# Order on three queues written out from a project's last two tiles to the next swiglu's first pair, at two borders; modulation off late tiles

## The chip, the cores and the metric

The kernel runs on one core of a Trainium2 chip. A core has five engines that run their own queues of instructions and meet at semaphores: PE (TensorE, matrix products out of SBUF into PSUM), DVE (VectorE), ACT (ScalarE), POOL (GpSimd) and SP (SyncE, which here issues the DMAs that bring the weights). The metric is the device time of one execution in microseconds; lower is better. Every time below is in microseconds unless it is marked ns.

## What is computed

The reference is a two-layer transformer on 256 tokens with 256 context tokens beside them, model width 1024, everything in float32. Layer 0 is a half-weighted swiglu, a short convolution mixer and another half-weighted swiglu; layer 1 is the same with attention in the place of the convolution. Each of the six blocks is preceded by a normalisation with modulation and followed by a gated addition:

```python
mod = (jax.nn.silu(c) @ mod_w[i] + mod_b[i]).reshape(bsz, 3, 3, 1, D_MODEL)
h = _rms(t, g) * (1 + scale) + shift           # before each block
y = (jax.nn.silu(gte) * up) @ w2               # gte, up = split(h @ w13), 2816 wide each
lat = lat + 0.5 * mod[:, 0, 2] * y             # a swiglu; a mixer has no 0.5
```

The context tokens go through layer 0 and the first swiglu of layer 1 as well, so up to there every product has 512 columns: 256 tokens (half 0) and 256 context tokens (half 1).

## The kernel before, in words

**Number format.** Each float32 operand is split into a high part (rounded to the format PE multiplies in) and a low part (what is left). `split` (L107) makes both: ACT writes the high part (L108) and DVE subtracts it from the source for the low part (L109). A product is three matmuls (`mm3`, L127): high weight by high data, high weight by low data, low weight by high data (L131, L132, L133). Weights come in as raw float32 tiles `wr` of 128 x 1024, 512 KB each, from a ring of 8 buffers, and are split into `wh` and `wl`, rings of 4 (`half`, L111).

**Swiglu.** A swiglu has 22 hidden tiles of 128, in three thirds of 8, 7 and 7 (`ffn`, L754). In each third the hidden tiles are computed first and then `project` (L569) adds their share to the eight output tiles of x, one after the other. Most hidden tiles go by a scheme with seven block products in place of eight (`Pair`, L675): it needs sums of the data's blocks (T1 to T4, made by `Blocks.sums`, L399) and of the weights' blocks (S1 to S4, `Pair.sums`, L696). Per hidden tile that is `head` (A11 and A12 by the data's blocks), `five` (S1 by T1), `six` (S2 by T2, S4 by the block B11), `seven` (S3 by T3) and `four` (A22 by T4). The last two of a tile run among the products of the next tile.

**Normalisation.** x cannot be normalised before its last tile is added. `finish` (L547) adds a product to x (L553, DVE), `square_add` (L247) squares it on ACT and adds the squares up on DVE. For the last two output tiles, 6 and 7, `project` computes the 256 columns of half 0 first for both, and then half 1 (`late`), so that half 0 can be normalised while half 1 is multiplied. The sum over partitions, its root and the broadcast back are `rms_sum` (L268, L273, L277) and `rms_all` (L283). Then DVE scales a tile of x (L295), ACT adds the shift (L384 for the high part, L389 for a raw copy that the sums need) and DVE makes the low part (L385). `tail_norm` (L504) queues these steps in `pending`, which `flush` lets out between products.

**The borders.** Called border 1 below: from the convolution's output projection (`cw_out`) to layer 0's second swiglu. Border 2: from that swiglu to the first of layer 1. Border 3: from that one to attention. After borders 1 and 2 the first two hidden tiles are computed plainly (`w13_mm`, L634, half 0 of tile 0, half 0 of tile 1, then half 1 of both), because T1 to T4 are not there yet; the third is the first `Pair`.

**Modulation.** mod is computed on DVE out of weights that stream in: one unit (L173, `next_unit`, L200) multiplies a 128 x 1024 tile by silu(c) and sums it up, 224 units in all. `tick(n)` (L210) asks for n units after a tile: in `project` after each tile (1.5, 1.7 or 2), elsewhere by other numbers.

**What sets the order.** The kernel is traced into a tile framework, whose scheduler places the instructions on each engine's queue by its own estimate; it may move a unit of modulation to another place than its `tick`. Inside `tc.manual_schedule` the named engines take the instructions of the block in the order in which they are written; others may still be placed between them. `tc.issue_after(i)` keeps a block's instructions behind i on i's engine. Each engine works through its queue in order.

## Time and profile before

| | us |
|---|---|
| median of 3 runs | 1569.25 |
| the three runs | 1569.25, 1573.82, 1568.98 |
| the profiled execution, its time | 1571.47 |
| its span, first to last instruction | 1569.7 |
| PE busy | 1557.7 |
| DVE busy | 1333.4 |
| ACT busy | 733.8 |

The profile is one execution. A row of a timeline gives start, duration, engine, line, operation, output and inputs, shape, count, and in brackets the idle time ahead of it with what ended it. Instructions of an engine overlap: the next one starts before the last has ended, so the step from start to start is what an instruction costs its queue, and it is shorter than the duration. A matmul of 256 columns is such a case. PE's busy time is modelled from matmul ends. "PEclk" is the clock that was granted to PE as a share of full speed.

### The profile page before, as it was taken

The page shows a single profiled execution, that of the slowest core. Times are in us where ns is not written, and L with a number is a line of the kernel's source. Part 1 is how long each engine was busy: PE and PEld are TensorE (multiplying, and loading weights), DVE is VectorE, ACT ScalarE, POOL GpSimd, SP SyncE. Part 2 cuts the span into 40 slices and gives each one's busy share as a digit, 9 for nine tenths or more (in the row PEclk, how much of TensorE's full clock was granted, in tenths as well). Part 3 has the DMA queues.
Part 4 walks back from the last instruction along what each step waited for, and adds up shares of the span by engine and source line. Part 5 has one row for each costly group of instructions (what it writes and reads, how often), then busy time and mean ns, then how long its engine had stood idle before and what let it go on. Part 6 is the DMA issues. An engine that isn't in the chain of part 4 may idle for free.

```text
span 1569.7 us, 25671 instructions
## 1 busy us (share of the span) xinstructions
PE 1557.7 (99%) x10210; PEld 1422.0 (91%) x10210; DVE 1333.4 (85%) x2129; ACT 733.8 (47%) x1213; POOL 25.4 (2%) x20
## 2 busy tenths in 40 slices
PE   9999999999999999999999999999999999999999
PEld 7888998999888899989899899999899889898888
DVE  5998789899997698978989989969978887887676
ACT  5622452545322365435345465435345445674553
POOL 0000000000000000000000000000000002300000
PEclk9999999999999999999999999999999999999999
DMA  9675246355565323542533614533733853366562
GB/s 373 224 237 180 89 132 187 107 173 159 194 209 166 114 75 108 177 146 87 189 126 117 196 41 135 187 108 118 239 112 114 265 154 106 123 207 221 171 199 75
DMA packets 72120, 248.80 MB, mean 159 GB/s; under 512 B 9024, under 2 KB 10816, under 8 KB 72000
## 3 DMA queue, kind: packets, MB, share of 16 engines
q1 hardware_dynamic: 69408, 245.40, 48.0%
q10 hardware_dynamic: 2592, 1.76, 0.4%
q8 instruction: 80, 1.31, 0.3%
q14 instruction: 40, 0.33, 0.1%
HBM read 244.77 MB, written 1.05 MB: 157 GB/s over the span
## 4 chain that ended last, share of the span: by engine, by line
PE 88%; DVE 6%; DMA 2%; ACT 2%; issue 1%; POOL 0%; POOLq 0%; SPq 0%; ACTq 0%; DVEq 0%
PE py L131 8%; PE py L132 8%; PE py L133 8%; PE p L131 6%; PE p L133 6%; PE p L132 6%; PE q L133 5%; PE q L131 4%; PE q L132 4%; PE py L139 2%; PE pu L139 2%; PE pg L139 2%; PE pg L132 1%; PE pg L133 1%; DMA wr<-in_w 1%; PE pu L132 1%
## 5 line engine op out<-in xcount | busy, mean ns | idle before, releaser
L108 ACT ACTIVATE wh<-wr 128x1024 fp32r<-128x1024 f32 (+2 forms) x442 | 393.7, 916 | 361.9 <-PE py L132 119.6
L109 DVE TENSOR_TENSOR wl<-wr,wh 128x1024 fp32r<-128x1024 f32 (+2 forms) x442 | 454.5, 1048 | 95.1 <-ACT wh L108 76.2
L173 DVE CUSTOM_DVE_ANT_0 junk<-wr,scbc,modb 128x1024 bf16<-128x1024 f32 x218 | 279.4, 1282 | 15.2 <-DMA wr<-in_modT 13.1
L131 PE MATMUL py<-gh,wh 128*128 128x512 f32 (+1 forms) x570 | 214.7, 377 | 0.0
L132 PE MATMUL py<-gl,wh 128*128 128x512 f32 (+1 forms) x570 | 214.0, 375 | 0.0
L133 PE MATMUL py<-gh,wl 128*128 128x512 f32 (+1 forms) x570 | 213.9, 375 | 0.0
L133 PEld LDWEIGHTS py<-gh,wl 128*128 128x128 f32 x570 | 108.3, 190 | 19.0
L131 PEld LDWEIGHTS py<-gh,wh 128*128 128x128 f32 x570 | 108.5, 190 | 18.4
L132 PEld LDWEIGHTS py<-gl,wh 128*128 128x128 f32 x570 | 108.5, 190 | 18.2
L131 PE MATMUL p<-th,wh 128*128 128x256 f32 x432 | 122.3, 283 | 0.0
L132 PE MATMUL p<-tl,wh 128*128 128x256 f32 x432 | 122.3, 283 | 0.0
L133 PE MATMUL p<-th,wl 128*128 128x256 f32 x432 | 122.2, 283 | 0.0
L553 DVE SCALAR_TENSOR_TENSOR x<-py,G,x 128x256 f32<-128x256 f32 x189 | 83.5, 479 | 36.3 <-PE py L133 25.1
L133 PE MATMUL q<-bh,wl 128*128 128x256 f32 x320 | 91.5, 286 | 0.1
L131 PE MATMUL q<-bh,wh 128*128 128x256 f32 x320 | 90.9, 284 | 0.4 <-ACT wh L108 0.4
L132 PE MATMUL q<-bl,wh 128*128 128x256 f32 x320 | 90.5, 283 | 0.0
L132 PEld LDWEIGHTS p<-tl,wh 128*128 128x128 f32 x432 | 82.8, 192 | 0.3
L131 PEld LDWEIGHTS p<-th,wh 128*128 128x128 f32 x432 | 82.8, 192 | 0.3
L133 PEld LDWEIGHTS p<-th,wl 128*128 128x128 f32 x432 | 82.8, 192 | 0.0
L108 ACT ACTIVATE w4h<-wr 128x512 fp32r<-128x512 f32 x54 | 33.8, 625 | 75.1 <-DMA wr<-in_w 56.9
L108 ACT ACTIVATE gh<-gm 128x512 fp32r<-128x512 f32 x66 | 41.6, 630 | 56.0 <-DVE gm L751 53.8
L711 DVE TENSOR_TENSOR wr<-wr,wr 128x1024 f32<-128x1024 f32 x54 | 66.0, 1222 | 0.7
(303 smaller groups left out, 3946.3 us busy)
## 6 DMA issues: line engine op xcount, KB each, us to landing
wr<-in_w SPq DMA_DIRECT2D x176, 512.0 KB, 4.5
wr<-in_modT SPq DMA_DIRECT2D x122, 512.0 KB, 4.5
wr<-in_w2b SPq DMA_DIRECT2D x64, 448.0 KB, 3.9
wr<-in_w2a SPq DMA_DIRECT2D x32, 512.0 KB, 4.7
pm<-in_mod SPq DMA_DIRECT2D x16, 512.0 KB, 10.2
wr<-in_cw_cx SPq DMA_DIRECT2D x16, 512.0 KB, 4.7
wr<-in_cw_b SPq DMA_DIRECT2D x8, 512.0 KB, 4.4
wr<-in_cw_out SPq DMA_DIRECT2D x8, 512.0 KB, 3.9
```

Of the source, the lines that this page charges most:

```text
L108: nc.scalar.activation(out=hi, in_=src, func=AF.Copy)
L109: return nc.vector.tensor_tensor(out=lo, in0=src, in1=hi.bitcast(F32), op=ALU.subtract)
L131: nc.tensor.matmul(ps, wh, mh, start=first, stop=False, **kw)
L132: nc.tensor.matmul(ps, wh, ml, start=False, stop=False, **kw)
L133: nc.tensor.matmul(ps, wl, mh, start=False, stop=last, **kw)
L139: nc.tensor.matmul(ps, w[0], m[2], start=first and n == 0, stop=False)
L173: nc.vector.tensor_tensor_reduce(out=junk, in0=raw[j], in1=scbc[:, v, :], scale=1.0, scalar=modb[:, l, col : col + 1], op0=ALU.mult, op1=A ...
L553: nc.vector.scalar_tensor_tensor(out=x[:, m, s * S : s * S + S], in0=ps[:, o : o + S], scalar=g[:, m, s : s + 1], in1=x[:, m, s * S : s * ...
L711: tt(out=v(r2), in0=v(r2), in1=s2.unsqueeze(1).to_broadcast([P, 2, T2]), op=ALU.subtract,)
```

## The change

At borders 1 and 2 the order on PE, DVE and ACT is written out, from the product of output tile 6 up to the head of the first `Pair` (`enter`). `project` with `hold` returns a `Late` in place of its last two tiles; `enter` takes their steps one by one: `mm` a product, `x` the addition to x, `sq` and `acc` the square and its addition, `rms` the sum and root. `sc` scales a tile (DVE), `hr` and `hi` write its raw copy and its high part (ACT), `lo` its low part (DVE); `two` splits two tiles at once from the raw copy; `hi_of` and `lo_of` are the two halves of `split`. The first two hidden tiles of a swiglu run in pieces of some of their eight k. A later `Pair` makes its weights (`weights`) behind the block's last DVE instruction, `edge`. T3 and T4, made before ahead of the second `Pair`, are now made inside its `weights`, after its S1 and S2.

Besides: `project` calls `tick` for output tiles 0 to 5 alone (0 to 4 where the last two are late), with larger numbers (1.6 to 2.4). The 0.5 of a swiglu's gate moves into the modulation's units (`scale`, and `modb` halved once), which takes away four small multiplications, and a gate is asked for by output tile, so that only the units of the tiles so far have to be done. The table of silu is loaded by a small activation written into the order.

```diff
+    def hi_of(hi, lo, src):
+        nc.scalar.activation(out=hi, in_=src, func=AF.Copy)
+    def lo_of(hi, lo, src):
+        return nc.vector.tensor_tensor(out=lo, in0=src, in1=hi.bitcast(F32), op=ALU.subtract)
...
-            scale=1.0,
+            scale=0.5 if ch in (2, 8) else 1.0,
...
     def gate_of(l, j):
-        m = mod_ready(l, 3 * j + 2)
-        if j == 1:
-            return m
-        t = const.tile([P, KT, 2], F32, name=f"G{l}{j}", tag=f"G{l}{j}")
-        nv = 1 if (l, j) == (1, 2) else 2
-        nc.vector.tensor_scalar(
-            out=t[:, :, :nv], in0=m[:, :, :nv], scalar1=0.5, scalar2=None, op0=ALU.mult
-        )
-        return t
+        ch = 3 * j + 2
+        def get(m):
+            while done.get((l, ch), 0) < (m // 2 + 1) * 2 * streams(l, ch):
+                next_unit()
+            return modv[l, ch]
+        return get
...
             if n == 0:
                 tt(out=b11, in0=b12, in1=b11, op=ALU.subtract)
-                keep("T1", b11)
-            elif n == 1:
+                self.t["T1"] = hot("th"), hot("tl")
+                return *self.t["T1"], b11
+            if n == 1:
                 tt(out=b12, in0=b22, in1=b12, op=ALU.add)
+                return
+            if n == 2:
                 tt(out=b22, in0=b22, in1=b11, op=ALU.add)
-                keep("T2", b22)
-            else:
-                tt(out=b21, in0=b21, in1=b22, op=ALU.subtract)
-                keep("T3", b12)
-                keep("T4", b21)
+                self.t["T2"] = hot("th"), hot("tl")
+                return *self.t["T2"], b22
+            tt(out=b21, in0=b21, in1=b22, op=ALU.subtract)
+            keep("T3", b12)
+            keep("T4", b21)
...
+        def begin(self, s, A, B, ri):
+            self.par, self.ts = (A, B, ri), {}
+            for hf in range(2):
+                self.raw[hf, s] = hot("hr", F32)
+                self.t["B", hf, s] = hot("bh"), hot("bl")
...
+        def sc(self, s, *ks):
+            for k in ks:
+                self.ts[k] = scaled(s, k, self.par[0], self.par[2])
...
+        def hr(self, s, *ks):
+            for k in ks:
+                hf, c = self.cols(k)
+                self.put(s, k, self.raw[hf, s][:, c])
+        def hi(self, s, k):
+            hf, c = self.cols(k)
+            self.put(s, k, self.t["B", hf, s][0][:, c])
+        def lo(self, s, k):
+            hf, c = self.cols(k)
+            hi, lo = (t[:, c] for t in self.t["B", hf, s])
+            nc.vector.scalar_tensor_tensor(
+                out=lo, in0=self.ts[k], scalar=self.par[1][:, k, s : s + 1],
+                in1=hi.bitcast(F32), op0=ALU.add, op1=ALU.subtract,
+            )
+        def two(self, s, k, part):
+            hf, c = self.cols(k, 2)
+            t = self.t["B", hf, s]
+            (lo_of if part else hi_of)(*(u[:, c] for u in (*t, self.raw[hf, s])))
...
+    class Late:
+        def __init__(self, products, ws, nk, gate):
+            self.products, self.ws, self.nk, self.gate = products, ws, nk, gate
+            self.ps, self.parts = {}, {}
+        def mm(self, i, s, k0=0, k1=None):
+            if k0 == 0:
+                self.ps[i, s] = psum("py")
+            self.products(
+                self.ps[i, s], self.ws[i], range(k0, k1 or self.nk), s * S, s * S + S
+            )
+        def x(self, i, s):
+            finish(6 + i, self.ps[i, s], s * S, s * S + S, self.gate, None)
...
+        def rms(self, s):
+            return rms_sum(s, (accs[s], self.parts[1, s]))
...
-            tick(ev)
+            if m < (5 if late else 6):
+                tick(ev)
         if late:
             wl = [get(m) for m in (6, 7)]
             if tail:
                 ready()
+            if hold:
+                return Late(products, wl, nk, gate)
...
+        def own(self):
             ts = half()
             for i, key in enumerate(("A11", "A12")):
                 self.w[key] = [t[:, i * T2 : i * T2 + T2] for t in ts]
-                split(*self.w[key], self.raw[i][:, T2:])
+                yield *self.w[key], self.raw[i][:, T2:]
         def keep(self, keys, part):
-            hi, lo = half()
-            split(hi, lo, part)
+            ts = half()
             for i, key in enumerate(keys):
-                self.w[key] = [t[:, i * T2 : i * T2 + T2] for t in (hi, lo)]
+                self.w[key] = [t[:, i * T2 : i * T2 + T2] for t in ts]
+            return *ts, part
...
+        def sum1(self):
+            r1, r2 = self.raw
+            nc.vector.tensor_tensor(
+                out=r1[:, :T2], in0=r1[:, :T2], in1=r2[:, :T2], op=ALU.subtract
+            )
+        def sum2(self):
+            r1 = self.raw[0]
+            nc.vector.tensor_tensor(
+                out=r1[:, T2:], in0=r1[:, T2:], in1=r1[:, :T2], op=ALU.subtract
+            )
+            return self.keep(("S1", "S2"), r1)
...
+        def weights(self):
+            for t in self.own():
+                split(*t)
+            split(*self.sums(0))
+            if "T3" not in self.h.t and not isinstance(self.h, FirstBlocks):
+                self.h.sums(3)
+            split(*self.a22())
+            split(*self.sums(1))
...
+    def enter(late, l, b, h, gs):
+        A, B = scale_of(l, 2 * b), mod_ready(l, 6 * b)
+        src = a["w13"][l, b]
+        w = [load_w(src[0])]
+        raw = [load_raw(src[1, :, c : c + 1024]) for c in (0, 1024)]
+        pr = Pair(src[2], h)
+        gs.extend(new_pair("g") for _ in range(2))
+        pp = []
+        def g(i, s, k0, k1):
+            if (s, k0) == (0, 0):
+                pp.append((psum("pg"), psum("pu")))
+            w13_mm(pp[i], w[i], h, range(k0, k1), s * S, s * S + S)
...
+        queues = (nc.tensor, nc.vector, nc.scalar)
+        with tc.manual_schedule(engines={e.engine for e in queues}):
+            late.mm(0, 0)
+            late.x(0, 0)
+            late.sq(0, 0)
+            late.acc(0)
+            late.mm(1, 0)
+            late.x(1, 0)
+            late.sq(1, 0)
+            late.mm(0, 1, 0, 5)
+            ss = late.rms(0)
+            late.mm(0, 1, 5)
+            late.x(0, 1)
+            late.mm(1, 1, 0, 1)
+            ri = rms_all(*ss)
+            late.mm(1, 1, 1)
+            ts = [half() for _ in raw]
+            w.append(lambda o, wd=P: tuple(t[:, o % 1024 : o % 1024 + wd] for t in ts[o // 1024]))
+            w1 = [(*t, r) for t, r in zip(ts, raw)]
+            hi_of(*w1[0])
+            h.begin(0, A, B, ri)
+            h.sc(0, 0)
+            h.sc(0, 1)
+            h.hi(0, 0)
+            h.hr(0, 0)
+            h.lo(0, 0)
+            h.sc(0, 2)
+            h.hi(0, 1)
+            late.sq(0, 1)
+            h.hr(0, 1)
+            h.lo(0, 1)
+            late.acc(1)
+            late.x(1, 1)
+            h.sc(0, 3)
+            h.hi(0, 2)
+            late.sq(1, 1)
+            h.lo(0, 2)
+            h.hi(0, 3)
+            h.lo(0, 3)
+            h.hr(0, 2)
+            g(0, 0, 0, 3)
+            lo_of(*w1[0])
+            ss = late.rms(1)
+            g(0, 0, 3, 4)
+            h.hr(0, 3)
+            hi_of(*w1[1])
+            g(1, 0, 0, 1)
+            ri1 = rms_all(*ss)
+            g(1, 0, 1, 4)
+            h.sc(0, 4, 5)
+            h.hr(0, 4, 5)
+            h.two(0, 4, 0)
+            h.sc(0, 6, 7)
+            h.two(0, 4, 1)
+            h.hr(0, 6, 7)
+            h.two(0, 6, 0)
+            lo_of(*w1[1])
+            h.two(0, 6, 1)
+            g(0, 0, 4, 8)
+            silu()
+            g(1, 0, 4, 8)
+            h.begin(1, A, B, ri1)
+            h.sc(1, 0, 1)
+            h.hr(1, 0, 1)
+            h.two(1, 0, 0)
+            pr.sum1()
+            h.sc(1, 2, 3)
+            h.two(1, 0, 1)
+            h.hr(1, 2, 3)
+            h.two(1, 2, 0)
+            h.sc(1, 4, 5)
+            h.two(1, 2, 1)
+            g(0, 1, 0, 4)
+            h.hr(1, 4, 5)
+            h.two(1, 4, 0)
+            h.sc(1, 6, 7)
+            h.two(1, 4, 1)
+            h.hr(1, 6, 7)
+            h.two(1, 6, 0)
+            t1 = h.sums(0)
+            h.two(1, 6, 1)
+            g(0, 1, 4, 8)
+            hi_of(*t1)
+            a22 = pr.a22()
+            hi_of(*a22)
+            lo_of(*t1)
+            own = list(pr.own())
+            for o in own:
+                hi_of(*o)
+            h.sums(1)
+            t2 = h.sums(2)
+            for o in own:
+                lo_of(*o)
+            p0 = post(0)
+            hi_of(*t2)
+            s12 = pr.sum2()
+            hi_of(*s12)
+            g(1, 1, 0, 8)
+            p0 = mul(0, *p0)
+            lo_of(*t2)
+            lo_of(*s12)
+            lo_of(*a22)
+            hi_of(*p0)
+            s34 = pr.sums(1)
+            lo_of(*p0)
+            p1 = post(1)
+            hi_of(*s34)
+            lo_of(*s34)
+            p1 = mul(1, *p1)
+            pr.head()
+            hi_of(*p1)
+            pr.edge = lo_of(*p1).ins
+        return pr
...
                 if t == 0 and not gs:
-                    w = [load_w(a["w13"][l, b, 0])]
-                    gs = [new_pair("g") for _ in range(2)]
-                    pp = [(psum("pg"), psum("pu")) for _ in range(2)]
-                    w13_mm(pp[0], w[0], h, range(KT), 0, S)
-                    flush()
-                    w.append(load_w(a["w13"][l, b, 1]))
-                    w13_mm(pp[1], w[1], h, range(KT), 0, S)
-                    h.sums(0)
-                    w13_mm(pp[0], w[0], h, range(KT), S, T2)
-                    w13_post(pp[0], gs[0], 0, T2)
-                    heads.append(Pair(a["w13"][l, b, 2], h))
-                    h.sums(1)
-                    heads[0].sums(0)
-                    w13_mm(pp[1], w[1], h, range(KT), S, T2)
-                    w13_post(pp[1], gs[1], 0, T2)
-                    heads[0].head()
-                    h.sums(2)
-                    heads[0].sums(1)
+                    heads.append(enter(late, l, b, h, gs))
...
-                        pr.sums(0)
-                        pr.sums(1)
+                        with tc.issue_after(prev.edge) if prev and prev.edge else nullcontext():
+                            pr.weights()
...
+    for ch in (2, 8):
+        b = modb[:, :, ch * KT : ch * KT + KT]
+        nc.vector.tensor_scalar(out=b, in0=b, scalar1=0.5, scalar2=None, op0=ALU.mult)
...
-    ffn(0, 0, h, T2, lazy_gate(0, 0), tail_norm(0, 1, hn), gs0, 2)
+    ffn(0, 0, h, T2, gate_of(0, 0), tail_norm(0, 1, hn), gs0, (2.3, 2.1))
...
-    hn = Blocks()
-    project(
+    late = project(
         by_pairs("cw_out"), lambda k, c0, c1: (zs[k][0][:, c0:c1], zs[k][1][:, c0:c1]), KT,
-        lazy_gate(0, 1), tail_norm(0, 2, hn), T2, 2, 1.5,
+        gate_of(0, 1), tail_square, T2, 2, hold=True, ev=1.6,
     )
-    h = hn
-    hn = Blocks()
-    ffn(0, 1, h, T2, lazy_gate(0, 2), tail_norm(1, 0, hn), (), 1.7)
-    h = hn
+    late = ffn(0, 1, Blocks(), T2, gate_of(0, 2), tail_square, late=late, hold=True, ev=(2.3, 1.8))
     hn = Plain()
-    ffn(1, 0, h, T2, lazy_gate(1, 0), tail_norm(1, 1, hn), (), 1.5)
+    ffn(1, 0, Blocks(), T2, gate_of(1, 0), tail_norm(1, 1, hn), late=late, ev=(2.4, 1.9))
```

## The prediction, made before the changed kernel ran

> **What bounds the kernel now.** I read the page first, then the busy time of a few stretches, then the timelines of PE, DVE and ACT in them, and last the order in which the changed program stands on each queue.

> ```profile
> span 1569.7 us, 25671 instructions
> PE 1557.7 (99%) x10210; PEld 1422.0 (91%) x10210; DVE 1333.4 (85%) x2129; ACT 733.8 (47%) x1213; POOL 25.4 (2%) x20
> ...
> PE 88%; DVE 6%; DMA 2%; ACT 2%; issue 1%; POOL 0%; POOLq 0%; SPq 0%; ACTq 0%; DVEq 0%
> ...
> wr<-in_w SPq DMA_DIRECT2D x176, 512.0 KB, 4.5
> ```

> PE is busy all the time but 12.0 us, and the chain is PE's for 88%, with DVE next. So a change that leaves PE's matmuls alone can win only PE's waits. The next view has four stretches: border 1 from the first late product to the second pair, border 2 likewise, and border 3 in two parts. Columns: stretch, length, busy time (count) of each engine, clock, DMA.

> ```profile
> 547.50:600.00 52.50, 51.23 (x417) 50.09 (x416) 48.19 (x74) 33.53 (x58) 0.00 (x0) 1.00 0.26 82
> 900.60:950.00 49.40, 48.69 (x400) 47.85 (x399) 43.22 (x66) 34.58 (x59) 0.00 (x0) 1.00 0.18 59
> 1256.00:1260.00 4.00, 2.48 (x20) 2.27 (x19) 3.08 (x5) 0.42 (x1) 0.00 (x0) 0.96 0.39 124
> 1260.00:1267.00 7.00, 7.00 (x36) 7.00 (x36) 4.51 (x14) 2.93 (x6) 0.00 (x0) 0.54 0.43 128
> ```

> PE is idle for 1.27 at border 1 and 0.71 at border 2, while DVE is busy for 92% and 87%. DVE is the second bound there: whatever is put on it, or makes it wait, soon reaches PE. Border 3 costs more: 1.52 idle, and then 7.0 us at a clock of 0.54, which is 7.0 x 0.46 = 3.2 more.

> PE's timeline around three waits, with the steps that the sum needs:

> ```profile
> 573.62 0.28 PE L131 MATMUL pu<-bh,wh 128*128 128x256 f32 x1
> 573.74 0.28 PE L132 MATMUL pu<-bl,wh 128*128 128x256 f32 x1
> ...
> 574.34 0.28 PE L131 MATMUL pu<-bh,wh 128*128 128x256 f32 x1
> 575.63 0.39 PE L132 MATMUL pg<-bl,wh 128*128 128x256 f32 x1 [1.01 <-DVE bl L109]
> ...
> 943.29 0.39 PE L131 MATMUL q<-bh,wh 128*128 128x256 f32 x1 [0.39 <-ACT wh L108]
> ...
> 1258.60 0.38 PE L268 MATMUL ss<-ones,acc 128*128 128x1 f32 x2 [1.52 <-DVE acc L259]
> ```

> A matmul of 256 columns is a step of 0.12. The wait at 575.63 took 1.29 - 0.12 = 1.17 from PE, 0.16 more than its idle time; short waits show only in this way. With some eight waits at border 1 and six at border 2, I put what PE loses there now at 1.27 + 8 x 0.16 = 2.6 and 0.71 + 6 x 0.16 = 1.6 (estimates; the idle time alone is the low end). Together 4.2 is all that the written order can win.

> **The change part by part.** Steps from start to start, which the sums go by:

> ```profile
> 557.59 1.26 DVE L295 SCALAR_TENSOR_TENSOR t<-x,A,ss 128x256 f32<-128x256 f32 x3
> 558.76 0.87 DVE L385 SCALAR_TENSOR_TENSOR bl<-t,mod,bh 128x256 fp32r<-128x256 f32 x2
> ...
> 585.76 0.69 DVE L109 TENSOR_TENSOR gl<-gm,gh 128x512 fp32r<-128x512 f32 x1
> 586.37 1.22 DVE L109 TENSOR_TENSOR wl<-wr,wh 128x1024 fp32r<-128x1024 f32 x1
> 587.50 0.69 DVE L645 TENSOR_TENSOR gm<-sg,pu 128x512 f32<-128x512 f32 x1
> 588.10 1.22 DVE L109 TENSOR_TENSOR tl<-hr,th 128x1024 fp32r<-128x1024 f32 x1
> ...
> 1248.92 1.28 DVE L173 CUSTOM_DVE_ANT_0 junk<-wr,scbc,modb 128x1024 bf16<-128x1024 f32 x1
> 1250.13 0.08 DVE L173 DVE_READ_ACCUMULATOR2_ANT mod<- 128x1 f32 x1
> ...
> 562.02 1.05 ACT L108 ACTIVATE wh<-wr 128x1024 fp32r<-128x1024 f32 x1
> 562.97 1.29 ACT L389 ACTIVATE hr<-t,mod 128x256 f32<-128x256 f32 x3
> ...
> 556.53 0.71 PE L283 MATMUL ss<-ident,ri 128*128 128x128 f32 x4
> 557.00 0.36 PE L133 MATMUL py<-zh,wl 128*128 128x256 f32 x1
> ```

> DVE: 0.39 for 256 columns (1.17 for three), 0.61 for 512, 1.13 for 1024, 1.21 for a unit of modulation. ACT: 0.95 for a copy of 1024. The broadcast takes PE 0.47. Let B be the start of PE's product after the broadcast for half 0 (557.00 at border 1).

> *Same work.* PE has the same 9538 rows before and after, so its work costs 0. DVE has three splits of 1024 as six of 512, 6 x 0.61 - 3 x 1.13 = +0.3 per border, counted below. POOL is not touched.

> *Border 1, the head.* The written order puts the high copy of the second hidden tile's weights ahead of the first activation on ACT. Its buffer is that of the last projection weights, and in the built program it waits for the eighth product after B: B + 0.08 + 7 x 0.12 + 0.28 = B+1.2. The copy ends its step at B+2.2; the first high part then ends at B+2.7, and DVE's first low part at B+3.2. PE comes there at B + 0.08 + 21 x 0.12 = B+2.6. It waits for the high part and then for the low one, and for the third low part again, since DVE has by then to add x's last tile as well: 0.3 + 0.4 + 0.9, 1.7 with restarts. Bounds: 0 if the copy were early, 1.9 if it hides nothing. DVE stands still for 1.8 meanwhile. Before, ACT made the high parts first (next fence) and this copy at 562.02.

> ```profile
> 558.10 0.91 ACT L384 ACTIVATE bh<-t,mod 128x256 fp32r<-128x256 f32 x2 [1.82 <-DVE t L295]
> ...
> 570.47 2.83 DVE L295 SCALAR_TENSOR_TENSOR t<-x,A,ss 128x256 f32<-128x256 f32 x7 [2.50 <-PE ss L283]
> ...
> 591.09 1.22 DVE L109 TENSOR_TENSOR tl<-hr,th 128x1024 fp32r<-128x1024 f32 x1
> 592.65 2.43 DVE L109 TENSOR_TENSOR wl<-wr,wh 128x1024 fp32r<-128x1024 f32 x3 [0.35 <-ACT wh L108]
> ```

> *Border 1, the tail.* Before, DVE made T3 and T4 (588.10, 591.09) ahead of the second pair's weights (592.65). Now they stand behind them, behind `edge`, and behind a sum that waits for PE's S4 product. From B+0.3 to T3's low part DVE has 22 instructions of 256 columns, 21 of 512 and 12 of 1024: 8.6 + 12.8 + 13.6 = 35.0, so B+35.3 without a wait. PE comes to S3 by T3 after 192 products of the swiglu (23.0), twelve small matmuls of half 1 (estimate 1.4, at the broadcast's pace) and 84 products of the pairs (10.1): B+37.1. DVE may thus wait for 1.8 in all. I count 5.4: 1.8 at the head, 1.6 behind ACT's raw copies and high parts of half 0, 2.0 behind the high parts of S3/S4 and of the second hidden tile and behind S4. T3 is there at B+40.7; PE, already 1.7 late, wants it at B+38.8: 1.9. T4 and S1's low part follow, 2.27 against the 1.44 of twelve products: 0.8, of which the queue, with six to eight products of the next blocks put ahead, hides some 0.4. Sum 1.7 + 1.9 + 0.4 + 0.3 for restarts = 4.3, against 2.6 before: **+1.7** (from -2.6 if DVE waits for less than 1.8, to +3).

> *Border 2.* The copy waits for nothing here, since each projection weight has a buffer of its own and the one it takes is read for the last time before B. The head costs 0.5. But four units of modulation stand inside the block on DVE, two by T1 and T2 and two by S3/S4, moved there by the scheduler: 4 x 1.21 = 4.85. Their two loads stand in SP's queue ahead of the fifth tile's weights, so a sum of those, placed ahead of `edge`, waits for a load that starts when S3/S4 is made. It lands 4.5 later by the page's median, 3.56 of which DVE fills: up to 0.9, taken as 0.6. DVE to the second pair's first own weight: 8.6 + 18 x 0.61 + 10 x 1.13 + 4.85 + 0.3 = B+36.0, with waits of 1.9 behind ACT and this 0.6 B+38.5. PE comes at B + 0.08 + 18 x 0.12 + 23.0 + 1.4 + 60 x 0.12 + 0.5 = B+34.3: 4.2. To T3 there are 3 x 0.61 + 2 x 1.13 = 4.1 more against 2.9 of PE: 1.2; then 0.4 as above. Sum 0.5 + 4.2 + 1.2 + 0.4 + 0.2 = 6.5, against 1.6: **+4.9** (from -1.6 to +7).

> *Modulation.* All 224 units stay. At border 1 the four in the late tiles go; PE lost little by them, **-0.3**. At border 3 the order still shows four units at the same places, between the same loads: 0, though the change is described as taking them off. Elsewhere units move by a tile or two; PE's other waits are short, so 0, within 1 either way.

> *Gate and table.* Four small DVE multiplications less, two more; silu's table is loaded elsewhere on ACT. 0: ACT is 47% busy, and half 1's activations, next behind the load, are wanted some 4 us later.

> **Sum.** 1.7 + 4.9 - 0.3 = +6.3 on the profiled execution's 1571.47. That stands 2.2 above the median 1569.25; on the median the sum is **1575.6**.

> **The rivals.** *DVE keeps pace.* If its waits at the head are filled and the total stays below 1.8 at border 1 and its like at border 2, both borders' losses go: 1569.25 - 4.2 = 1565.1, faster. For it: DVE had 2.50 of idle time at 570.47 that the new order fills. Against it: the copy on ACT and the four units.

> *Border 3 clears.* If the modulation's loads land 1.5 earlier there, its 1.52 and 3.2 go: 1575.6 - 4.7 = 1570.9. Against it: the same places in both queues.

> *The clock halves at border 2.* Two waits of some 2 us lie 1.4 apart there, and border 3's row shows 0.54 after only 1.52 idle. That would cost up to 3.2: 1578.8. For it: that row. Against it: 1.01 idle at 575.63 left no mark, and DVE's lateness would cover part.

> [...]

> **How the numbers follow.** Forecast 0.50 (by itself 1572 to 1579), DVE keeps pace 0.20, border 3 clears 0.13, the clock 0.12, none of these 0.05. The range 1565 to 1580 takes in all four. This kernel's no change is within 0.3%, 1564.5 to 1574.0, about what a measurement can tell. Faster: half of the first rival and little else, 0.12. Same: its other half, border 3, and the forecast's low end, 0.28. Slower 0.60.

> **What would show it.** Right: at border 1 an ACT weight copy before the first high part, with DVE idle some 1.8; in both borders PE waits on `tl` (T3) and on the second pair's weights, about 2 at border 1 and 5 at border 2; four units between `hr` sums at border 2; the same stretch of low clock at border 3. Wrong: PE idle of less than 1 at either border, or DVE idle for long between T1 and T3.

## The result

The changed kernel takes 1582.01 us (median of 4 runs, 1580.04 to 1582.87), the kernel before 1569.55 beside it (4 runs, 1568.98 to 1573.82): ratio 1.0072, 95% interval 1.0052 to 1.0092. It is 12.5 slower, where 6.3 was forecast; 1582.01 lies above the range's 1580.

The page of the changed kernel, its profiled execution (1582.87):

```profile
span 1581.0 us, 25678 instructions
PE 1560.3 (99%) x10210; PEld 1421.9 (90%) x10210; DVE 1334.8 (84%) x2133; ACT 736.7 (47%) x1221; POOL 25.4 (2%) x20
...
PE 82%; DVE 11%; ACT 3%; DMA 3%; issue 1%; POOL 0%; POOLq 0%; ACTq 0%; DVEq 0%
```

The span is 11.3 longer, PE is busy for only 2.6 more, and DVE's share of the chain has gone from 6% to 11%: new waits of PE, mostly for DVE. The four stretches that answer to those of the prediction (stretch, length, busy time of PE, PEld, DVE, ACT, POOL with counts, clock, DMA share, GB/s):

```profile
549.80:604.90 55.10, 52.30 (x425) 51.06 (x424) 45.22 (x72) 33.75 (x61) 0.00 (x0) 1.00 0.17 58
906.20:961.00 54.80, 49.77 (x406) 48.62 (x405) 48.98 (x79) 35.09 (x62) 0.00 (x0) 1.00 0.22 72
1267.00:1271.50 4.50, 2.31 (x20) 2.11 (x18) 1.66 (x4) 0.27 (x1) 0.00 (x0) 1.00 0.49 187
1271.50:1278.00 6.50, 6.48 (x42) 6.48 (x43) 4.57 (x11) 3.35 (x7) 0.00 (x0) 0.74 0.46 164
```

PE is idle for 2.8 at border 1 and 5.0 at border 2; border 3 still has its wait (2.2) and a stretch of low clock behind it (0.74). PE's timeline at its longest waits:

```profile
565.76 0.39 PE L138 MATMUL pg<-bl,wh 128*128 128x256 f32 x1 [0.54 <-DVE bl L461]
...
601.14 0.39 PE L138 MATMUL p<-tl,wh 128*128 128x256 f32 x1 [1.90 <-DVE tl L109]
...
948.97 0.38 PE L137 MATMUL p<-th,wh 128*128 128x256 f32 x1 [1.88 <-ACT sg L841]
953.97 0.38 PE L139 MATMUL p<-bh,wl 128*128 128x256 f32 x1 [1.27 <-DVE wl L109]
958.04 0.39 PE L138 MATMUL p<-tl,wh 128*128 128x256 f32 x1 [1.43 <-DVE tl L109]
...
1271.52 0.38 PE L274 MATMUL ss<-ones,acc 128*128 128x1 f32 x2 [2.21 <-DVE acc L265]
```

Each takes 0.16 more from PE than its idle time, as in the prediction. To see where all of the 11.3 is, the trace's PE starts were added up by stage: the time from one start to the next, less the step of that form (0.120 for 256 columns, 0.227 for 512). What is left is PE's loss, in us. The same 560 matmuls stand for border 1 in every kernel, and so on; "half" is the part in which five or more matmuls in a row took about twice their step (0.21 where it is 0.120, as at 1273.70 in the changed kernel). Each row is one profiled execution; e1 to e12 are the runs below.

```
                 start  ffn00  conv  border 1    rest   border 2    rest  border 3    attn
                                     (half)     ffn01   (half)     ffn10  (half)
before           13.9   1.1    0.4   2.8         1.0    1.9         0.7   6.7 (2.7)   4.1
after            15.6   0.9    1.2   5.4         1.8    6.9         2.3   5.8 (1.2)   4.1
e1 order only    17.6   0.6    0.4   5.1         0.9    4.7         1.0   5.4 (0.9)   4.1
e2 modul. only   13.7   1.1    1.2   2.6         1.8    4.8         1.2   3.4         4.1
e3 bias late     13.7   1.0    1.2   7.6 (1.4)   2.4    7.4         1.5   5.4 (1.0)   4.1
e4 units out     14.2   0.6    1.2   5.7 (1.4)   2.0    4.5         2.0   7.0 (2.7)   4.1
e5 copy late     15.8   0.8    1.2   3.8         1.6    7.5         1.0   5.6 (1.2)   4.1
e6 T3 inside     15.7   1.1    1.2   5.4         2.7    9.7 (2.6)   2.5   3.2         4.1
e7 head first    13.8   1.4    1.2   5.8         1.7    7.2 (1.1)   1.1   3.4         4.1
e8 border 3      13.6   0.8    0.4   2.8         0.8    1.9         0.7   1.7         4.1
e9 T3 first      13.7   1.0    1.2   5.0         1.4    8.2 (1.5)   0.9   3.7         4.1
e10 border 0     15.8   1.1    0.1   6.3 (1.5)   1.8    8.8 (1.6)   0.9   5.4 (1.4)   4.1
e11 mended       15.7   0.6    0.4   4.1 (1.5)   2.9    4.6 (1.6)   1.0   1.7         5.4
e12 mended again 13.7   0.6    0.4   2.8         2.7    5.6 (1.6)   0.8   1.7         4.1
```

Before to after: border 1 +2.6, border 2 +5.0, and +3.2 in places that the forecast had at zero: the convolution +0.8, the rest of the two later swiglus +0.8 and +1.6. With the first swiglu's pairs (-0.2) that is 10.5 with the unrounded values. Start (+1.7) and border 3 (-0.9) vary between executions of one kind, as the runs show.

### The profile page after: what moved, and what is told of

It reads as the page before. It is cut to its first block, busy times and chain, and to the rows that moved or that the text cites. A ratio compares the mean times of both kernels' runs of the same rounds, so it can differ in the third digit from the quotient of the medians.

```text
span 1581.0 us, 25678 instructions
## 1 busy us (share of the span) xinstructions
PE 1560.3 (99%) x10210; PEld 1421.9 (90%) x10210; DVE 1334.8 (84%) x2133; ACT 736.7 (47%) x1221; POOL 25.4 (2%) x20
## 3 DMA queue, kind: packets, MB, share of 16 engines
HBM read 244.77 MB, written 1.05 MB: 155 GB/s over the span
## 4 chain that ended last, share of the span: by engine, by line
PE 82%; DVE 11%; ACT 3%; DMA 3%; issue 1%; POOL 0%; POOLq 0%; ACTq 0%; DVEq 0%
PE py L137 8%; PE py L138 8%; PE py L139 8%; PE p L137 5%; PE p L139 5%; PE p L138 5%; PE q L139 4%; PE q L137 3%; PE q L138 3%; DVE wl L109 3%; PE py L145 2%; PE pu L145 2%; PE pg L145 2%; ACT wh L108 1%; DMA wr<-in_w 1%
## 5 line engine op out<-in xcount | busy, mean ns | idle before, releaser
L108 ACT ACTIVATE wh<-wr 128x1024 fp32r<-128x1024 f32 (+2 forms) x430 | 383.4, 916 | 368.1 <-PE py L138 158.3
L109 DVE TENSOR_TENSOR wl<-wr,wh 128x1024 fp32r<-128x1024 f32 (+2 forms) x430 | 441.1, 1046 | 88.3 <-ACT wh L108 69.4
L607 DVE SCALAR_TENSOR_TENSOR x<-py,mod,x 128x256 f32<-128x256 f32 x213 | 94.2, 478 | 50.7 <-PE py L139 39.4
L795 DVE TENSOR_TENSOR wr<-wr,wr 128x1024 f32<-128x1024 f32 x54 | 65.9, 1221 | 0.9
L108 ACT ACTIVATE gh<-gm 128x512 fp32r<-128x512 f32 x62 | 39.0, 630 | 55.4 <-DVE gm L864 53.9
L139 PE MATMUL q<-th,wl 128*128 128x256 f32 x216 | 61.6, 285 | 1.2 <-DVE wl L109 1.1
## 6 DMA issues: line engine op xcount, KB each, us to landing
wr<-in_w SPq DMA_DIRECT2D x176, 512.0 KB, 4.3
wr<-in_modT SPq DMA_DIRECT2D x120, 512.0 KB, 4.6
wr<-in_w2a SPq DMA_DIRECT2D x32, 512.0 KB, 4.5
pm<-in_mod SPq DMA_DIRECT2D x16, 512.0 KB, 10.2
wr<-in_cw_cx SPq DMA_DIRECT2D x16, 512.0 KB, 4.6
wr<-in_cw_b SPq DMA_DIRECT2D x8, 512.0 KB, 4.4
wr<-in_cw_out SPq DMA_DIRECT2D x8, 512.0 KB, 3.8
```

Source lines behind the costliest of these rows:

```text
L108: nc.scalar.activation(out=hi, in_=src, func=AF.Copy)
L109: return nc.vector.tensor_tensor(out=lo, in0=src, in1=hi.bitcast(F32), op=ALU.subtract)
L139: nc.tensor.matmul(ps, wl, mh, start=False, stop=last, **kw)
L607: nc.vector.scalar_tensor_tensor(out=x[:, m, s * S : s * S + S], in0=ps[:, o : o + S], scalar=g[:, m, s : s + 1], in1=x[:, m, s * S : s * ...
L795: tt(out=v(r2), in0=v(r2), in1=s2.unsqueeze(1).to_broadcast([P, 2, T2]), op=ALU.subtract,)
```

## The experiments

### Which part of the change: e1, e2

e1 keeps the written order and takes the modulation's rates, rule, gates and halving back; e2 is the kernel before with that part of the change alone.

```diff
 e1, against the changed kernel
-            if m < (5 if late else 6):
-                tick(ev)
+            tick(ev)
...
-    late = ffn(0, 1, Blocks(), ..., late=late, hold=True, ev=(2.3, 1.8))
+    late = ffn(0, 1, Blocks(), ..., late=late, hold=True, ev=(1.7, 1.7))
 e2, against the kernel before
-            tick(ev)
+            if m < (5 if late else 6):
+                tick(ev)
```

> The written order alone, with the modulation's rates, gates and halving as they were before. The two theories share the table of what PE loses by stage (time from start to start beyond its own step): border 1 2.8 before and 5.4 after, border 2 1.9 and 6.9, start 13.9 and 15.6, the rest of the three swiglus and the convolution 3.3 and 6.2. Theory: the order by itself costs only DVE's lateness, and no unit of modulation stands in border 2's block here: border 1 5.4 to 5.9 (two units are back in its late tiles), border 2 2.0 to 2.6 (6.9 less the four units' 4.85), start 13.9, rest 3.3; about 1573, +3.3. Rival (the order itself is slow at border 2, and the units fill waits of DVE): border 2 5 to 7, about 1577.

> The modulation's part alone: rates, the rule that late tiles have no units, a gate made tile by tile, and the two halvings of the biases; the order at the borders is the scheduler's as before. Theory: the loss that the forecast had at zero comes from this part: start +1.7 (the halvings stand ahead of the first sum of squares on DVE), convolution and the rest of the two later swiglus +3.2, border 3 -0.9, border 1 -0.3; three units stand in border 2's block here too, +1.5 to +3.6. About 1574 to 1577. Rival (units cost nothing wherever DVE has spare time, and it is the written order that delays the tiles behind it): start +1.7 at most, elsewhere within 0.5, about 1570 to 1571.

e1: 1579.58 against 1569.71, ratio 1.0051 (1.0032 to 1.0070). e2: 1573.12, ratio 1.0019 (1.0006 to 1.0032). The stages of e1 are near the theory's for border 1 (5.1, where 5.4 to 5.9 was expected; four units are back there, not two) and right for the rest (as before), and wrong for border 2: 4.7, not 2.0 to 2.6. So the order alone costs 2.8 there, and two waits stay, on the second pair's weights and on T3. Its time is 6.6 above the theory's 1573: 2.1 to 2.7 of that is border 2, and its four executions had a mean clock of 0.9968 (the profiled one lost 17.6 at the start).

e2 is what the forecast missed: the modulation's part alone gives the convolution +0.8, the rest of the two swiglus +0.7 and +0.5, and +3.0 at border 2, where no order was written. Three units now stand among the steps of border 2 in the scheduler's order too (918.55, 926.51 and 944.03; before, none); what each costs there was not separated. The start did not lose the 1.7 that its theory said (13.7), border 3 fell further than its 0.9 (from 6.7 to 3.4, 2.7 of which is half clock), and the time, 1573.12, is below the theory's 1574 to 1577.

### The start: e3

```diff
         for step in FIRST_STEPS.split():
             steps[step[0]](*(int(c) for c in step[1:]))
+        for ch in (2, 8):
+            b = modb[:, :, ch * KT : ch * KT + KT]
+            nc.vector.tensor_scalar(out=b, in0=b, scalar1=0.5, scalar2=None, op0=ALU.mult)
...
-    for ch in (2, 8):
-        ...
```

> The changed kernel with the two halvings of the biases written behind the first block's steps. Theory: they delay the first sum of squares by 0.24, and the clock at the start falls for longer on that account (mean clock 0.79 to 0.87 from 10 to 20 us): start back to 13.9, 1.7 less, 1580.3. Rival (the clock at the start differs from run to run, whatever DVE does): start 15 to 16 again, 1582.

1583.66, ratio 1.0083 (1.0065 to 1.0101). The start came back to 13.7, as the theory has it, but e2 has 13.7 with the halvings in front, and e1 17.6 without any. So the rival holds: the start differs by execution. What differs is the clock: in the profiles with no half clock between 10 and 21 us the start loses 13.6 to 14.2, in those with 3.4 us of it 15.6 to 15.8, and in e1, with 6.8 us, 17.6. These are windows at the start of e1 and of e3 (0.50 and 1.00):

```profile
14.00:20.00 6.00, 6.00 (x42) 3.29 (x42) 1.93 (x5) 1.38 (x4) 0.00 (x0) 0.50 1.03 412
```

```profile
14.00:20.00 6.00, 5.74 (x49) 4.00 (x45) 4.24 (x12) 4.45 (x10) 0.00 (x0) 1.00 1.02 407
```

### The units in border 2's block: e4

The changed kernel's timeline at border 2, first DVE and then ACT:

```profile
945.15 1.27 DVE L179 CUSTOM_DVE_ANT_0 junk<-wr,scbc,modb 128x1024 bf16<-128x1024 f32 x1
...
946.35 1.22 DVE L795 TENSOR_TENSOR wr<-wr,wr 128x1024 f32<-128x1024 f32 x1
```

```profile
947.60 1.06 ACT L112 ACTIVATE wh<-wr 128x1024 fp32r<-128x1024 f32 x1 [2.74 <-DVE wr L795]
948.57 0.35 ACT L841 COPY sg<-p 128x256 f32<-128x256 f32 x1
```

A unit delays the sum of S3/S4 on DVE (L795); ACT stands still for it for 2.74, and the copy of the first pair's product, which needs neither, stands behind the high part of S3/S4 in ACT's queue. PE waits for that copy (948.97). e4 holds the units of the first third's pairs behind the block.

```diff
                     prev = pr
-                    tick(0.5)
+                    edge = pr.edge or edge
+                    with tc.issue_after(edge) if edge else nullcontext():
+                        tick(0.5)
```

> The changed kernel with the modulation units of the first third's pairs held behind the block's last low part on DVE, so that none stands in border 2's block. Theory (DVE sets border 2): its loss falls from 6.9 to 2.0 to 2.6, the waits on the copy of the first pair's product (2.0), on the second pair's weights (1.4) and on T3 (1.6) go together; the units reappear behind it and cost up to 1 in the pairs: about 1578.5. Rival (ACT's order is what PE waits for: the copy stands behind the high part of S3/S4): 2.0 stays, border 2 at 4 to 5, about 1580.

1580.11, ratio 1.0056 (1.0035 to 1.0077). The first wait goes, the other two stay: border 2 is 4.5. That is a number of the rival's (4 to 5), but the wait that the rival keeps is the one that went; of the theory's three waits one went. The timeline of e4, first DVE right behind the block and then PE at the two waits:

```profile
947.82 1.28 DVE L179 CUSTOM_DVE_ANT_0 junk<-wr,scbc,modb 128x1024 bf16<-128x1024 f32 x1
...
949.62 1.28 DVE L109 TENSOR_TENSOR wl<-wr,wh 128x512 fp32r<-128x512 f32 x2
```

```profile
950.36 0.39 PE L139 MATMUL p<-bh,wl 128*128 128x256 f32 x1 [1.05 <-DVE wl L109]
...
954.43 0.39 PE L138 MATMUL p<-tl,wh 128*128 128x256 f32 x1 [1.42 <-DVE tl L109]
```

A unit that was held came first behind the block, ahead of the second pair's weights, and its 1.20 is about the wait there (1.2 with the restart); e1 has one unit in the block and waits 1.4. The wait on T3 has another cause.

### The head of border 1: e5

The changed kernel's timeline at the head of border 1, first ACT and then DVE:

```profile
561.41 1.06 ACT L112 ACTIVATE wh<-wr 128x1024 fp32r<-128x1024 f32 x1 [2.67 <-PE py L138]
562.38 0.49 ACT L447 ACTIVATE bh<-t,mod 128x256 fp32r<-128x256 f32 x1
```

```profile
562.90 0.48 DVE L461 SCALAR_TENSOR_TENSOR bl<-t,mod,bh 128x256 fp32r<-128x256 f32 x1 [1.57 <-ACT bh L447]
```

```diff
             w1 = [(*t, r) for t, r in zip(ts, raw)]
-            hi_of(*w1[0])
             h.begin(0, A, B, ri)
...
             h.hi(0, 3)
+            hi_of(*w1[0])
             h.lo(0, 3)
```

> The changed kernel with ACT's copy of the second hidden tile's weights, which waits for PE's eighth product behind the broadcast, written behind the four high parts of half 0. Theory (the head's loss is this copy, and DVE's idle 1.57 behind it makes T3 late in turn): border 1's waits of 0.15, 0.40 and 0.70 at the head shrink to 0.4 together, DVE's 1.57 goes, and the wait on T3's low part falls from 2.06 to 1.3 to 1.7 (1.57 less for DVE, but PE comes 0.9 earlier): border 1 from 5.4 to 3.8 to 4.2. Rival (T3 is late from waits that DVE has further on, behind PE and ACT): the head goes, T3's wait grows to 2.9 by what the head gave: border 1 stays at 5.2 to 5.6.

1580.38 (one run); border 1 is 3.8. The three waits at the head (0.15, 0.40, 0.70) are gone, so the copy was their cause. The 3.8 is the theory's number, but partly by chance: the wait on T3 neither fell nor grew, and 0.3 came off the third pair's S1 instead (PE's timeline of e5):

```profile
599.97 0.39 PE L138 MATMUL p<-tl,wh 128*128 128x256 f32 x1 [1.90 <-DVE tl L109]
```

It is 1.90 of idle time here, in the changed kernel, in e1 (601.91) and in e7 (599.75); at border 2 it is 1.42 or 1.43 in the changed kernel, e1, e3, e4, e5 and e10. Neither theory said that: a lateness of DVE that has gathered on the way would change with PE's coming.

### T3: e6, e7, e9

e6 makes T3 and T4 inside the block (one line, `h.sums(3)` behind `lo_of(*s34)`). e7 moves the head of the first pair, with ACT's copy, ahead of the high part of S3/S4:

```diff
             p1 = post(1)
+            pr.head()
             hi_of(*s34)
             lo_of(*s34)
             p1 = mul(1, *p1)
-            pr.head()
```

> The changed kernel with T3 and T4 made inside the written block, behind the low part of S3/S4 and ahead of the second pair's weights. Theory (DVE has more to do than PE gives it time for, so the place of T3 only says on which tile PE waits): the waits on T3 (2.06 at border 1, 1.59 at border 2) go, and PE waits for the second pair's own weights, 3.4 later, in their stead: border 1 5.1 to 5.8, border 2 6.5 to 7.5. Rival (T3's place behind the second pair's weights is what costs): border 1 3.4, border 2 5.3, 3.6 less in all.

> The changed kernel with the head of the first pair, and with it ACT's copy of its product, written ahead of the high part of S3/S4. Theory (DVE sets border 2): the wait of 2.04 on that copy goes, PE comes to the second pair's weights 2.0 earlier, and the wait there grows from 1.43 to 3.2 to 3.5: border 2 6.5 to 7.2, border 1 as it was. Rival (the place in ACT's queue costs 2.0): border 2 4.7 to 5.2.

e6: 1584.29, one run. Border 1 5.4 and border 2 9.7, 7.1 without the stretch at half clock: the theory's numbers. At border 2 PE waits in T3's stead for the second pair's own weights (951.28), as the theory has it. But at both borders it also waits for ACT's copy of the first pair's product (596.41, 954.22), which now stands behind the high part of T4 in ACT's queue; the theory had no such wait. PE's timeline of e6, border 1 first:

```profile
596.41 0.39 PE L137 MATMUL p<-th,wh 128*128 128x256 f32 x1 [1.26 <-ACT sg L841]
...
951.28 0.39 PE L137 MATMUL p<-bh,wh 128*128 128x256 f32 x1 [3.08 <-ACT wh L108]
...
954.22 0.58 PE L137 MATMUL p<-th,wh 128*128 128x256 f32 x1 [1.91 <-ACT sg L841]
```

e7: 1578.42, one run. Border 2 is 7.2, and 6.1 without the half clock: between the two. The wait on the copy shrinks from 2.04 to 0.62, the one on the second pair's weights grows from 1.43 to 2.20, not to 3.2, and T3's there falls to 0.4. Border 1 is 5.8, for the third pair's S1 (1.19 against 0.82). PE's timeline of e7:

```profile
952.89 0.39 PE L139 MATMUL p<-bh,wl 128*128 128x256 f32 x1 [2.04 <-DVE wl L109]
```

What sets T3 stands on DVE in the changed kernel, here at border 1:

```profile
596.33 0.69 DVE L853 TENSOR_TENSOR sg<-q,sg 128x512 f32<-128x512 f32 x1 [0.34 <-PE q L139]
596.93 0.68 DVE L109 TENSOR_TENSOR wl<-wr,wh 128x512 fp32r<-128x512 f32 x1
597.53 0.68 DVE L803 TENSOR_TENSOR wr<-wr,wr 128x512 f32<-128x512 f32 x1
598.14 1.21 DVE L427 TENSOR_TENSOR hr<-hr,hr 128x1024 f32<-128x1024 f32 x1
599.27 0.68 DVE L809 TENSOR_TENSOR wr<-wr 128x512 f32<-128x512 f32 x1
599.87 2.35 DVE L109 TENSOR_TENSOR tl<-hr,th 128x1024 fp32r<-128x1024 f32 x2
```

The add at 596.33 waits for PE's own S4 product. From there five steps (3.5) and T3's low part (1.1) come to 601.0; PE has 24 products (2.9) until it needs it. Both are counted from the same product, so 601.0 - 599.1 = 1.9 whatever came earlier. e9 turns T4's sum (L427) and T3's low part round:

```diff
+            keep("T3", b12)
             tt(out=b21, in0=b21, in1=b22, op=ALU.subtract)
-            keep("T3", b12)
             keep("T4", b21)
```

> The changed kernel with one pair of steps turned round behind the block: the low part of T3 ahead of T4's sum on DVE, where the sum (1.14) stands ahead of both low parts. Theory, formed from the wait on T3, which was 2.06 in the changed kernel and in the runs with the copy late, with the order alone and with the head first, whenever PE came there: it is a chain behind PE's own S4 product, namely the add that waits for it, a weight's low part, a sum for the third pair, T4's sum and then T3's low part. Then the wait falls by 1.1 to 0.9 at border 1 and from 1.6 to 0.5 at border 2: border 1 4.2 to 4.5, border 2 5.6 to 6.0. Rival (DVE is late as a whole): PE waits for T4 or the third pair instead, border 1 5.2 to 5.6, border 2 6.6 to 7.1.

1578.10, one run. T3's wait falls to 0.3 at border 1 and is gone at border 2, more than expected, but 1.2 comes back on the second pair's S1 (PE's timeline of e9):

```profile
597.66 0.39 PE L138 MATMUL p<-tl,wh 128*128 128x256 f32 x1 [0.16 <-DVE tl L109]
...
601.13 0.39 PE L139 MATMUL q<-th,wl 128*128 128x256 f32 x1 [1.04 <-DVE wl L109]
```

Border 1 is 5.0 (4.2 to 4.5 expected, 5.2 to 5.6 by the rival), border 2 6.8 without the half clock, where the theory had 5.6 to 6.0 and the rival 6.6 to 7.1. So the chain behind S4 sets the wait on T3, as the theory says, but what the move wins comes back in good part on the next tile, as the rival says, at border 2 in full.

### The convolution: e10

```diff
         split(zs[m][0], zs[m][1], z)
-        tick(5)
+        with tc.issue_after(rows["late"]):
+            tick(5)
```

(`rows["late"]` is the last addition to x in `project`.)

> The changed kernel with the convolution's modulation units held behind the last update of x at the border ahead of it, which no order was written for. Theory: the new rates put units right ahead of the normalization there, and the convolution's 0.8 more comes from that: convolution from 1.2 to 0.4, the rest as in the changed kernel. Rival (the loss comes from the units inside the convolution, now denser): 1.0 or more.

1583.12, one run, with half clock at three borders. The convolution's loss is 0.1, less than the 0.4 of the kernel before. DVE's timeline ahead of its normalization, in the kernel before, in the changed kernel and in e10:

```profile
375.28 0.48 DVE L553 SCALAR_TENSOR_TENSOR x<-py,G,x 128x256 f32<-128x256 f32 x1 [0.31 <-PE py L133]
...
376.01 1.28 DVE L173 CUSTOM_DVE_ANT_0 junk<-wr,scbc,modb 128x1024 bf16<-128x1024 f32 x1
...
377.80 1.28 DVE L173 CUSTOM_DVE_ANT_0 junk<-wr,scbc,modb 128x1024 bf16<-128x1024 f32 x1
...
379.12 1.26 DVE L295 SCALAR_TENSOR_TENSOR t<-x,A,ss 128x256 f32<-128x256 f32 x3
```

```profile
376.35 1.27 DVE L179 CUSTOM_DVE_ANT_0 junk<-wr,scbc,modb 128x1024 bf16<-128x1024 f32 x1
...
377.55 0.48 DVE L607 SCALAR_TENSOR_TENSOR x<-py,mod,x 128x256 f32<-128x256 f32 x1
377.95 1.27 DVE L179 CUSTOM_DVE_ANT_0 junk<-wr,scbc,modb 128x1024 bf16<-128x1024 f32 x1
...
380.58 1.27 DVE L179 CUSTOM_DVE_ANT_0 junk<-wr,scbc,modb 128x1024 bf16<-128x1024 f32 x1
...
381.78 1.26 DVE L301 SCALAR_TENSOR_TENSOR t<-x,A,ss 128x256 f32<-128x256 f32 x3
```

```profile
380.22 1.26 DVE L301 SCALAR_TENSOR_TENSOR t<-x,A,ss 128x256 f32<-128x256 f32 x3 [0.80 <-PE ss L289]
```

With the units gone so is the loss. A unit right ahead of the scaling is not what is new, for the kernel before has one there too (377.80). What is new is a unit in front of the last addition to x that half 0's sum of squares needs (376.35 ahead of 377.55; before, the addition at 375.28 waits for PE alone). Counted from the same product of PE, the first scaling comes 1.16 later in the changed kernel than before, and in e10 0.67 earlier than before. The units come from the convolution's own `tick(5)`, and the scheduler placed them; which of them costs what was not separated. The rest of the two later swiglus has no such single place in the traces; which of the rate, the rule and the gate brings its +0.8 and +1.6 was not separated either.

### Border 3 in the kernel before: e8

```diff
-    tick(1)
+    with tc.issue_after(rows["late"]):
+        tick(1)
```

(and likewise for attention's other four ticks up to the heads)

> The kernel before, with the attention's first modulation units held behind the last update of x at border 3, so that none of them stands between the two last tiles, waiting for its load. Theory: PE's wait of 1.7 for the sum of squares goes, and with it the stretch of low clock behind it: border 3 from 6.7 to 1.5 to 2.5, and in all 1565 to 1567 by the median, less than the profile's 4.7 because the low clock does not follow in every execution (border 3 was 3.4 in the run with the modulation's part alone, with no low clock). Rival (the units are only moved and make the sum late behind them): border 3 at 3 to 5, 1568 to 1570.

1567.83 against 1569.57, ratio 0.9993 (0.9984 to 1.0003). At border 3 no wait for the sum of squares and no low clock are left (windows of e8):

```profile
1256.00:1262.00 6.00, 6.00 (x52) 5.94 (x51) 3.84 (x11) 3.56 (x9) 0.00 (x0) 1.00 0.01 3
1262.00:1268.00 6.00, 5.32 (x39) 4.74 (x39) 5.80 (x13) 3.19 (x7) 0.00 (x0) 1.00 0.03 5
```

The stage is 1.7, 5.0 less than in the profile of before, and 2.7 of the 5.0 is half clock in that one execution. The median is 1.7 lower, less than the 2.6 to 4.6 that 1565 to 1567 would be, and not told from nothing.

### The order mended: e11, e12

Both take e1 with the edits of e5, e7 and e8. e11 moves T3's low part into the block in the place of A22's and holds the pairs' units behind the second pair's weights; A22's low part is thereby taken after the sum of S3/S4 has changed its source, so that part of its computation is not the reference's. e12 leaves A22 and the units where they were and lets the second pair's weights go ahead of the second hidden tile's product:

```diff
 e12
             hi_of(*p0)
+            t3 = h.t3()
+            hi_of(*t3)
             s34 = pr.sums(1)
...
             hi_of(*s34)
             lo_of(*s34)
+            pr.edge = lo_of(*t3).ins
             p1 = mul(1, *p1)
             hi_of(*p1)
-            pr.edge = lo_of(*p1).ins
+            lo_of(*p1)
```

> The written order with the modulation's old rates and gates, and five steps mended: the copy behind the high parts, the first pair's head ahead of the high part of S3/S4, T3's low part inside the block in the place of A22's, the pairs' units behind the second pair's weights, and the attention's units behind the last update of x at border 3. Theory (the losses of the written order are these single places): border 1 1.0 to 2.0 (2.8 before), border 2 1.9 to 3.0 (1.9 before), border 3 1.5 to 2.5, rest 3.3: 1565 to 1568, 2 to 4 under the kernel before. Rival (the written order is bound by DVE as a whole, and each wait that is mended comes back behind it): border 1 3.5 to 4.5, border 2 4 to 5: 1569 to 1572.

> The written order with the modulation's old rates and gates, mended once more: the copy behind the high parts, the first pair's head ahead of the high part of S3/S4, T3 made inside the block behind the low part of S3/S4 (A22's low part stays where it was), the second pair's weights free to stand ahead of the second hidden tile's product, and the attention's units behind the last update of x at border 3; the pairs' units are not held any further. Theory (single places, each mended without putting units elsewhere): border 1 1.3 to 2.3, border 2 1.8 to 2.8, border 3 1.5 to 2.0, convolution, the rest of the two swiglus and attention as before (0.4, 0.9, 0.8, 4.1): 1566 to 1569 by the median, 1 to 3 under the kernel before, less if the low clock follows at a border. Rival (DVE as a whole is the bound: waits return on the second pair's S1 and S2, 1.1 and 0.9 as in the run before): border 1 3.5 to 4.5, border 2 4 to 5, 1570 to 1572.

e11: 1574.32 against 1571.36, ratio 1.0025 (1.0016 to 1.0035). Without the half clock border 1 is 2.6, above the theory's 1.0 to 2.0, and border 2 3.0, at its end; and the units that were held back came later, in the rest of the second swiglu (2.9) and in attention (5.4). The time is above both ranges. e12: 1570.16 against 1571.39, ratio 0.9992 (0.9984 to 1.0001). The time is that of the kernel before, but not because the written order costs nothing now: border 1 is 2.8 as before, border 2 4.0 without the half clock against 1.9, the rest behind border 1 2.7 against 1.0, and border 3's edit gives back what these lose. Beside e8, the kernel before with the same edit at border 3, the profile of e12 loses about 4 more without the half clock; the medians, each against the kernel before beside it, do not show that (0.9992 and 0.9993). Border 1 lies between the theory's 1.3 to 2.3 and the rival's 3.5 to 4.5, border 2 and the time are the rival's, and the waits that are left at the two borders are the pair that the rival names, first on the second pair's S1 from ACT and then from DVE (PE's timeline of e12):

```profile
597.38 0.38 PE L137 MATMUL q<-th,wh 128*128 128x256 f32 x1 [1.08 <-ACT wh L108]
598.83 0.39 PE L139 MATMUL q<-th,wl 128*128 128x256 f32 x1 [0.71 <-DVE wl L109]
...
950.91 0.38 PE L137 MATMUL q<-th,wh 128*128 128x256 f32 x1 [1.08 <-ACT wh L108]
952.36 0.51 PE L139 MATMUL q<-th,wl 128*128 128x256 f32 x1 [0.71 <-DVE wl L109]
```

## Why the prediction was wrong

The sign was right and border 2 came out as forecast, that one partly by chance; the sum was half of what came. The main step that failed is the 0 for everything outside the borders, and the next is the tail of border 1. By its steps:

**Same work** (0): right; the page has 10210 matmuls on PE in both kernels (9538 stands in no view).

**Border 1, the head** (1.7): right in its mechanism, 1.25 in size (0.15 + 0.40 + 0.70), shown by e5.

**Border 1, the tail** (T3 1.9, S1's low part 0.4): 2.06 and 0.38 measured, and 0.82 more on the third pair's S1, which it did not have. Its reason for T3 was wrong: DVE's total lateness from B to T3, with 1.8 from the head in it. e5 took the head away and T3's wait stayed at 2.06; it is a chain behind PE's S4 product. That the same number came out is chance.

**Modulation off border 1's late tiles** (-0.3): 0.2 in the scheduler's order (e2, 2.6 against 2.8), not seen in the written one: e1, which has four units there again, loses 5.1, not more than 5.4. Border 1 in all: +1.4 forecast, +2.6 measured.

**Border 2** (+4.9): +5.0. Its 4.2 up to the second pair's head came in two waits, 2.04 on ACT's copy and 1.43 on the second pair's weights, and T3's 1.2 as 1.59. The four units were named rightly as a cost, but they are about half of it, as far as these runs take them out: held behind the block (e4) or placed otherwise (e1) they give back 2.4 and 2.2, not the 4.85 that they take on DVE. One then stands ahead of the second pair's weights, where PE still waits for 1.2 and 1.4, and T3's 1.58 stays in both, so it is the chain behind S4 here too. That the sum was met to 0.1 is partly chance.

**Border 3** (0): its units and its wait stayed (2.37 of loss against 1.68). That the profile has 5.8 against 6.7 is the clock's (1.2 of half clock against 2.7).

**Elsewhere** (0, within 1 either way): this is the step that failed. It is +3.2: convolution 0.8, the rest of the two swiglus 0.8 and 1.6; e2 shows 2.0 of it without the written order, so that much is the modulation's new rates, rule and gates, and e10 shows that the convolution's comes from the units. The argument was that units move by a tile or two and that PE's other waits are short. But a unit is 1.2 on DVE, and moving it by a tile can put it in front of a step that PE waits for, as ahead of the convolution, a border that was not looked at. For the rest of the two swiglus the places stay open.

**The clock** (a rival, 0.12): it did not halve at border 2 in the profile of the changed kernel, so the sum held without it. It did in e6, e7 and e9 to e12 there, and at border 1 in e3, e4, e10 and e11, for 1.1 to 2.6. The forecast had it as all or nothing; it is a part of some executions.

Of the measured 12.5, the stages other than the start and border 3 give 10.5. Of the other 2.0 the clock fits 0.8: 61 executions of the kernel before, beside e1 to e12, had a mean of 0.9985, the four of the changed kernel 0.9980. What is left, 1.2, is within the spread of four runs on each side and was not explained.

## What to carry to other kernels

When units of filler work lose their places, ask at each of the new places what stands behind them on that queue: here a unit of 1.2 came to stand in front of an addition that a sum of squares needs, and that stage lost 0.8 more, at a border that the change did not touch, because the scheduler was free to move units there. In an order written by hand, look for a step that waits for an engine whose next need is counted from the same event: such a wait is the same however early all else is (1.90 or 1.91 of idle time in seven profiles), and a shorter chain mends it (0.16 in e9). And hold filler behind the last step that needs the border's result, which took border 3 from 4.0, or 6.7 with the half clock, to 1.7 in the profiles; the medians do not tell that from nothing.

## What the runs showed of the hardware

```profile
594.07:597.48 3.41, 2.33 (x20) 2.13 (x18) 3.41 (x5) 2.47 (x4) 0.00 (x0) 1.00 0.00 0
597.48:600.89 3.41, 2.70 (x21) 2.49 (x22) 3.37 (x5) 0.94 (x1) 0.00 (x0) 1.00 0.00 0
```

```profile
949.05:952.47 3.42, 1.63 (x12) 1.22 (x11) 3.42 (x5) 1.81 (x2) 0.00 (x0) 1.00 0.00 0
952.47:955.88 3.41, 3.41 (x17) 3.41 (x18) 3.41 (x5) 1.96 (x3) 0.00 (x0) 0.50 0.33 91
```

At border 1 the edge at 597.48 falls between the two waits, and PE is busy for 2.33 and 2.70 of the two windows; the clock stays at 1.00. At border 2 both waits lie in one window, PE is busy for 1.63 of it, and the next one runs at 0.50. At the three borders of the 14 traces PE is busy for less than half of a window 14 times, and 13 times the next window ran at half clock (the other is the changed kernel's 945.52 to 948.93, with 1.57 busy). Between 0.50 and 0.56 it was three of five, above that one (e1's 1266.22 to 1269.64, with 0.68). At the start and the end of the kernels it is less clear: at the start the clock also fell behind windows with 0.72 to 0.91 (0.91 in the changed kernel, 3.11 us of 10.26 to 13.68). So PE's busy time in a window, which is modelled, does not tell by itself whether half clock follows, and why some stretches of half clock last two windows (1259.64 to 1266.47 in the kernel before) is not shown. In e12 at border 2 the half clock came behind 1.79 us of idle time in two pieces, inside one window.

Where the windows lie against the first instruction differs from trace to trace: beside the changed kernel's, e12's are 0.12 later (949.05 against 948.93) and e1's 0.15 earlier (1266.22 against 1273.20 less two windows, 1266.37). That a kernel's time thereby has a part that is drawn anew each time is the author's estimate; what was measured is that the time goes with the mean clock. The 61 executions of the kernel before, by mean clock: 11 at 1.000 took 1568.1 on average, 18 at 0.999 took 1569.7, 20 at 0.998 took 1571.0, 12 at 0.997 took 1573.1. Each 0.001 is about 1.7 us, close to the span times 0.001. A wait at a border thus cost itself and, in some of the profiles, 0.9 to 2.7 us more (the brackets of the table of stages); and a comparison of a few runs should be read with their clocks beside it.
